# Two-operand scores for strided attention groups, their steps moved into the gate projections, and roots on other engines at both ends

## The chip, the cores and the metric

The kernel runs on one core of one Trainium2 chip. The metric is the device time of one execution in microseconds (us). A core has TensorE (PE in the profile: matmuls and transposes; PEld its weight loads), VectorE (DVE), ScalarE (ACT), GpSimd (POOL) and SyncE (SP, which mainly issues transfers).

## The reference

One layer of an encoder block on 512 tokens of 1024 features, in float32. All weights are read once.

```python
x = x + 0.5 * rmsnorm(swiglu(rmsnorm(x, g1), gate1, up1, down1), g2)      # D_FF = 2816
h = rmsnorm(x, g3)
qa, ka, va, qb, kb, vb, gate_a, gate_b = split(h @ w_in)
ya = neighbourhood_attention(qa, ka, va, rpb) @ w_branch_a                 # 8 heads of 64
yb = dilated_mixture(qb, kb, vb, slopes) @ w_branch_b                      # 3 groups of 4 heads of 64
merged = sigmoid(gate_a) * ya + sigmoid(gate_b) * yb
x = x + rmsnorm(merged @ w_out, g4)
x = x + 0.5 * rmsnorm(swiglu(rmsnorm(x, g5), gate2, up2, down2), g6)
```

The dilated mixture has groups 0, 1 and 2 with dilations 1, 4 and 16. Each group computes a softmax over its own keys with a distance bias (`s - slope * distance`), and the three groups of a head position are weighted by a softmax over their log-sums. rmsnorm divides by the root of the mean square over the 1024 features.

## The kernel before

**Numbers in two parts.** Every matmul operand is split into a rounded high part (ScalarE: a copy that rounds) and a low part (VectorE: source minus high part); `split` does both. `mm3` (lines 203 to 205) multiplies high by high, high by low and low by high. A projection of one 128-feature piece over all tokens is 8 x 3 matmuls with 512 moving columns (`proj_into`).

**Order.** The program is written as one stream; a planner (the framework's scheduler, with a simulated timeline) then orders the instructions of each engine and places waits. In a few stretches PE, ScalarE and VectorE are pinned to the written order (`ordered`): from the start to the first standard pair of the first feed-forward, around the end of the feed-forward and mixing stages, and at the end of the kernel. Elsewhere the planner may move an instruction ahead of others that aren't ready. SBUF work tiles come from one pool of 54 units of 128x512 (`unit`), PSUM tiles from a pool of 8 banks (`bank`), and weight pieces from a pool of 12.

**Start.** Four token tiles of x (128 tokens each) are loaded. For tiles 0 and 1 the sum of squares comes from ScalarE (and for one half of tile 0 from VectorE), then GpSimd adds epsilon and raises to the power -0.5 (`start`, lines 1477 to 1490), VectorE scales (`scaled`), PE transposes (`turned`, line 314) and ScalarE and VectorE write the high and low parts of `hn` (lines 317 and 318). A few matmuls on an idle tile keep PE's clock up (`keep_warm`, counts in `WARM`).

**Feed-forward.** `first_products` runs four products over the first 256 tokens while tiles 2 and 3 are still being turned (`turn_rows`); each turned tile keeps its PSUM bank until `keep` (line 325) has copied it once more into the "whole" tiles. These copies are queued in `kept` and, before the change, run behind the fourth product. Then come two standard projections and `seven`, a seven-product scheme over blocks of two features. `down` is the same for the way back, and `rows_out` normalises, adds and, in the last stage, stores.

**Mixing.** Projections of queries and keys alternate with attention steps that wait in a queue `pend`; `step(n)` takes n steps off it. For each head there is a score step (`scores`, through `g_sc` for the dilated groups), a transpose step (`g_tr`: scales the probabilities, then PE transposes, line 1049) and a value step (`g_pv`, `attend`). `joint(g)` reads the statistics of all three groups back from memory and computes the weights that `g_tr` scales by; the statistics are written by a transfer on ScalarE's queue when a group's last head has been scored. In groups 1 and 2 a block of 128 queries has 128 keys: per block one matmul with the keys' high part and one with their low part, 128 moving columns each, into one quarter of a bank (lines 1017 and 1018). Then VectorE adds the bias table and takes the minimum, and ScalarE takes the exponential. In group 0 and in the neighbourhood attention a block has 256 keys.

Before the change, the steps taken around the far and near values (`v_far`, `v_near`) and a last `step(len(pend))` empty `pend` before the gates. The 16 gates (`gate`, one projection and a sigmoid on ScalarE each) then carry 26 transpose, weight and value steps, two behind each gate from the second on. After them the branch product (`br`) sums ten features' worth of heads per output piece: heads of the neighbourhood attention are rows 0 to 3, group 0 rows 4 and 5, group 1 rows 6 and 7, group 2 rows 8 and 9.

**End.** The last token tile gets its root from GpSimd (`rstd_of`); VectorE does three of the four last multiplies, ScalarE and GpSimd the fourth, and SP and ScalarE issue two stores each.

Of the kernel before, what the change touches and what calls it, by code (L numbers as in the profile page):

```python
# [40 lines left out]
WARM = (0, 1, 0, 1, 9, 2)  # L41
# [4 lines left out]
def block_kernel(ctx, tc, x, gains, weights, rpb_near, rpb_all, alibi0, alibi12, out):  # L46
# [21 lines left out]
    def bank(name="ps"):  # L68
        return pp.tile([P, 512], F32, tag="ps", name=name)
# [47 lines left out]
    staged = {}  # L117
    loads = deque()
# [12 lines left out]
    def convert(n, raw=None):  # L131
        if n in staged:
            hi, lo = [wp.tile([P, PIECE], F32R, tag="w", name="w") for _ in range(2)]
            for u, cs in zip(staged.pop(n), halves):
                split(hi[:, cs], lo[:, cs], u)
# [118 lines left out]
    def first_products(turns, early):  # L254

        w = [take(False) for _ in range(EARLY)]
# [3 lines left out]
        for i in range(EARLY):  # L260
# [11 lines left out]
            if i in turns:  # L272
                turn_rows()
                fetch()
            g = unit(name="g")
# [3 lines left out]
        while kept:  # L279
            kept.popleft()()  # L280
# [18 lines left out]

    def pre_norm(t, g, ss):  # L300
# [5 lines left out]
        late.append(lambda: [turned(t, b, xs[b]) for b in range(2)])  # L306

# [168 lines left out]
    def rows_out(acc, ks, turn, one, ends, g_post, f, g_pre, store, src=None, pin=True):  # L476
# [23 lines left out]
        for tb in complete:  # L500
            squares_of(*tb)
        for tb in complete:
            weighted(*tb)
# [5 lines left out]
        for t in range(NT):  # L509
# [11 lines left out]
            r = rstd_of(ss[t], f)  # L521
            if store and t == NT - 1:

                for b, i in ((1, 0), (0, 0), (0, 1), (1, 1)):
                    part = slice(i * 256, i * 256 + 256)
                    g, o = fg[t][b][:, part], xu[t][b][:, part]
                    if b > i:
                        nc.scalar.mul(g, g, r)
                        nc.gpsimd.tensor_tensor(o, g, o, op=ALU.add)
                    else:  # L530
                        nc.vector.scalar_tensor_tensor(o, g, r, o, op0=ALU.mult, op1=ALU.add)
                for b, i in ((0, 0), (0, 1), (1, 0), (1, 1)):
                    c0 = b * 512 + i * 256
                    (nc.sync, nc.scalar)[i].dma_start(out_r[:, t, c0:c0 + 256], xu[t][b][:, i * 256:i * 256 + 256])
# [11 lines left out]
    def ffn(g, store, src):  # L546
# [34 lines left out]
        if store:  # L581
            nc.scalar.activation(small("ms"), mhalf, AF.Silu)
# [302 lines left out]
    def qk_parts(kind, pq, pk):  # L885
# [3 lines left out]
        for par in range(2):  # L889
            own = slice(par * 64, par * 64 + 64)  # L890
            other = slice(64 - par * 64, 128 - par * 64)
            q, kh, kl = unit(F32R), unit(F32R), unit(F32R)
# [4 lines left out]
            for cols, v in order_k(kind, pk[own]):  # L897
                split(shaped(kh[own, cols], v), shaped(kl[own, cols], v), v)
# [17 lines left out]
    def v_near():  # L916
# [13 lines left out]
        for n in (1, 2, 3, 0):  # L930
# [8 lines left out]
            step()  # L939
        return [vv[3]] + vv[:3]  # L940

    def v_far(g):
# [13 lines left out]
        for n in range(4):  # L956
# [4 lines left out]
            if n % 2:  # L961
                step()
# [35 lines left out]
    def windows(wide, kT, i):  # L998
        if not wide:
            return kT[:, i * P:(i + 1) * P]  # L1000
# [659 lines left out]
```

## Time and profile before

| what | value |
|---|---|
| median of 3 runs | 1087.01 us (1086.24 to 1088.82) |
| the profiled execution | 1087.04 us, span 1085.3 us |
| granted clock of TensorE | 0.999 |
| busy | PE 99%, PEld 89%, DVE 77%, ACT 61%, POOL 17% |
| chain that ended last | PE 93%, DVE 2%, DMA 2%, ACT 1% |
| DMA | 189.82 MB, mean 175 GB/s |

Times in a timeline are microseconds from the span's start. A row of the timeline has start, length, engine, line, operation, output<-inputs, shape and count, and in brackets how long the engine was idle before it and what ended that. Lengths of matmuls are modelled and overlap; what a matmul costs PE is read from one start to the next. A row of the waits says who waited at which line for whom: total us, times, longest. A row of the groups has count, busy us, mean ns of one, and idle time before them. A row of the windows gives, for a stretch, busy us and instructions of PE, PEld, DVE, ACT and POOL, then the granted clock, the DMA share and GB/s.

### The profile page before, as it was taken

To read this page: it belongs to the slowest core of one execution; us is meant where nothing else is said; L and a number is where in the kernel's file an instruction comes from. 1 tells how busy PE (TensorE), PEld (TensorE's weight loads), DVE (VectorE), ACT (ScalarE), POOL (GpSimd) and SP (SyncE) were. 2 spreads that over 40 slices of the span, in tenths; PEclk is the share of its full clock that TensorE was granted. 3 is DMA by queue.
4 is the path that set the end of the run, shared out by engine and by line. 5 is a ranking of instruction groups with operands and counts; after the bars stand their busy time and mean duration, and the time that the engine had idled before them with its cause. 6 is when DMAs were issued, how large, how long until landed. Compare 5 with 4: busy or idle time off the path is not lost.

```text
span 1085.3 us, 18420 instructions
## 1 busy us (share of the span) xinstructions
PE 1073.0 (99%) x6689; PEld 967.6 (89%) x6689; DVE 834.2 (77%) x1561; ACT 657.1 (61%) x1334; POOL 182.2 (17%) x252
## 2 busy tenths in 40 slices
PE   8999999999999999999999999999999999999997
PEld 6899999998888988888988888889899999998876
DVE  7988777768997679876467654777988777778975
ACT  7646555565784767767656651376656555565762
POOL 4112111014333000000000001133302111114301
PEclk9999999999999999999999999999999999999999
DMA  9889997569993353422232239666928767859962
GB/s 338 184 202 248 225 233 186 143 160 280 237 292 98 127 194 109 134 87 79 70 103 79 79 111 304 161 113 207 277 64 211 190 162 188 203 184 240 218 199 77
DMA packets 95725, 189.82 MB, mean 175 GB/s; under 512 B 24081, under 2 KB 26641, under 8 KB 95634
## 3 DMA queue, kind: packets, MB, share of 16 engines
q1 hardware_dynamic: 68320, 134.18, 37.1%
q0 software_dynamic: 24624, 54.01, 27.6%
q8 instruction: 52, 0.85, 0.3%
q10 hardware_dynamic: 2690, 0.46, 0.2%
q14 instruction: 39, 0.32, 0.1%
HBM read 183.58 MB, written 7.58 MB: 176 GB/s over the span
## 4 chain that ended last, share of the span: by engine, by line
PE 93%; DVE 2%; DMA 2%; ACT 1%; issue 1%; POOL 0%; SPq 0%; DVEq 0%; POOLq 0%; ACTq 0%
PE ps L203 11%; PE ps L204 11%; PE ps L205 11%; PE q L203 10%; PE q L204 10%; PE q L205 10%; PE p L203 4%; PE p L204 3%; PE p L205 3%; PE r L205 2%; PE r L204 2%; PE r L203 2%; PE c L205 2%; PE c L204 2%; PE c L203 2%; PE ps L1049 1%
## 5 line engine op out<-in xcount | busy, mean ns | idle before, releaser
L113 DVE TENSOR_TENSOR w<-raw,w 128x512 fp32r<-128x512 f32 (+1 forms) x136 | 122.9, 909 | 69.7 <-ACT w L112 69.4
L112 ACT CAST w<-raw 128x512 fp32r<-128x512 f32 (+1 forms) x136 | 107.8, 799 | 83.5 <-PE ps L204 41.9
L203 PE MATMUL ps<-hn,w 128*128 128x512 f32 (+1 forms) x408 | 155.5, 381 | 2.3 <-ACT whole L325 2.3
L205 PE MATMUL ps<-hn,w 128*128 128x512 f32 (+1 forms) x408 | 153.2, 375 | 0.0
L204 PE MATMUL ps<-hn,w 128*128 128x512 f32 (+1 forms) x408 | 153.1, 375 | 0.0
L113 DVE TENSOR_TENSOR w<-t,w 128x512 fp32r<-128x512 f32 x160 | 108.9, 688 | 20.9 <-ACT w L112 18.4
L112 ACT CAST w<-t 128x512 fp32r<-128x512 f32 x160 | 97.6, 619 | 42.8 <-DVE t L380 24.3
L203 PE MATMUL p<-v,w 128*128 128x256 f32 x320 | 90.6, 283 | 0.3 <-ACT up L454 0.3
L203 PEld LDWEIGHTS ps<-hn,w 128*128 128x128 f32 x408 | 76.9, 189 | 15.3 <-ACT whole L325 2.7
L203 PE MATMUL q<-v,w 128*128 128x256 f32 x320 | 90.6, 283 | 0.0
L204 PE MATMUL p<-v,w 128*128 128x256 f32 x320 | 90.5, 283 | 0.0
L204 PE MATMUL q<-v,w 128*128 128x256 f32 x320 | 90.5, 283 | 0.0
L205 PE MATMUL p<-v,w 128*128 128x256 f32 x320 | 90.2, 283 | 0.0
L205 PE MATMUL q<-v,w 128*128 128x256 f32 x320 | 89.9, 283 | 0.0
L205 PEld LDWEIGHTS ps<-hn,w 128*128 128x128 f32 x408 | 76.8, 188 | 14.0
L204 PEld LDWEIGHTS ps<-hn,w 128*128 128x128 f32 x408 | 77.0, 189 | 12.5
L374 POOL DMA_DIRECT2D t<-in_weights_dram x40 | 35.0, 875 | 287.4 <-DVE w L113 85.3
L204 PE MATMUL q<-hn,w 128*128 128x256 f32 x288 | 81.5, 283 | 0.0
L205 PE MATMUL q<-hn,w 128*128 128x256 f32 x288 | 81.5, 283 | 0.0
L203 PE MATMUL q<-hn,w 128*128 128x256 f32 x288 | 81.3, 283 | 0.0
L203 PE MATMUL q<-w,a 128*128 128x512 f32 x192 | 75.0, 391 | 0.6 <-DVE part L831 0.6
L204 PE MATMUL q<-w,a 128*128 128x512 f32 x192 | 74.7, 389 | 0.0
(269 smaller groups left out, 3018.6 us busy)
## 6 DMA issues: line engine op xcount, KB each, us to landing
raw<-in_weights_dram SPq DMA_DIRECT2D x90, 512.0 KB
t<-in_weights_dram SPq DMA_DIRECT2D x88, 256.0 KB
t<-in_weights_dram POOLq DMA_DIRECT2D x80, 256.0 KB, 5.6
w<-in_weights_dram SPq DMA_DIRECT2D x40, 256.0 KB
rows<-in_weights_dram SPq DMA_DIRECT2D x32, 256.0 KB
w<-in_weights_dram POOLq DMA_DIRECT2D x32, 256.0 KB, 6.2
tb<-in_weights_dram POOLq DMA_DIRECT2D x12, 512.0 KB, 8.5
rows<-in_weights_dram POOLq DMA_DIRECT2D x24, 256.0 KB, 11.3
```

Source lines behind the costliest of these rows:

```text
L112: nc.scalar.copy(hi, src)
L113: nc.vector.tensor_tensor(lo, src, hi.bitcast(F32), op=ALU.subtract)
L203: nc.tensor.matmul(o, sh, mh, start=start, stop=False, **kw)
L204: nc.tensor.matmul(o, sh, ml, start=False, stop=False, **kw)
L205: nc.tensor.matmul(o, sl, mh, start=False, stop=stop, **kw)
L374: nc.gpsimd.dma_start(t1, weights[gate][:, :512], accum_op=ALU.add)
L1049: nc.tensor.transpose(ps[:, i * P:(i + 1) * P], s, ident)
```

## The change

1. **Scores of groups 1 and 2** (`scores_narrow`): the keys of two query blocks lie in one tile, high parts in its first half and low parts in its second. One matmul per block with 256 moving columns (128 high, 128 low) gives both products side by side. VectorE adds the low products and the bias table into a new tile `low`, then adds the high products and takes the minimum. A head now takes 4 matmuls instead of 8 and two banks instead of one.
2. **Steps**: `v_near` takes two steps instead of four, the second part of `v_far` none, and `pend` isn't emptied before the gates. Four steps (scores of three heads of group 2, and `joint(1)`) move behind gates 1 and 2, and the others two gates later. The branch product takes rows 4 and 5 last.
3. **Turned tokens**: at the start all transposes come before the copies out of PSUM, and the copies are ordered by half: both tiles' first halves, then the second (`turned_first`). The `keep` copies run behind a turn inside `first_products` instead of behind the fourth product.
4. **Roots**: tiles 0 and 1 and the last tile of the kernel get their root from ScalarE (`Sqrt`) and a reciprocal on VectorE, instead of GpSimd's power. The first table load is that of Sqrt; the Silu load moves behind the first turn of the first feed-forward, and another Sqrt load is placed ahead of the last stage's tail. At the end VectorE does all four multiplies, each followed by its store.
5. **Smaller ones**: the low half of one staged weight piece moves to GpSimd; the row of gains and the ones it is multiplied by get 128 rows (zeros but for one) instead of one; the warm-up counts grow.

The diff, cut to its core:

```diff
@@ -38,7 +38,7 @@
 EXTRA = "e"
-WARM = (0, 1, 0, 1, 9, 2)
+WARM = (1, 2, 1, 1, 10, 3)
 PINNED = (mybir.EngineType.PE, mybir.EngineType.Activation, mybir.EngineType.DVE)
@@ -253,6 +256,8 @@
+        if turns[0] == 0:
+            nc.scalar.activation(small("ms"), mhalf, AF.Silu)
         w = [take(False) for _ in range(EARLY)]
@@ -272,12 +277,14 @@
                 fetch()
+                if i == 1:
+                    nc.scalar.activation(small("ms"), mhalf, AF.Silu)
+                while kept and i != 1:
+                    kept.popleft()()
             g = unit(name="g")
             early.append((o, g))
-        while kept:
-            kept.popleft()()
@@ -297,6 +304,14 @@
+    def root_of(ss, f):
+        c, m, r = small("ms0"), small("ms"), small("rstd")
+        nc.gpsimd.tensor_scalar_add(c, ss[:, 0:1], f * EPS)
+        nc.scalar.activation(m, ss[:, 1:2], AF.Sqrt, bias=c)
+        nc.vector.reciprocal(r, m)
+        return r
     def pre_norm(t, g, ss):
@@ -304,6 +319,18 @@
         late.append(lambda: [turned(t, b, xs[b]) for b in range(2)])
+    def turned_first(t, b, xs):
+        pt = bank()
+        for i in range(4):
+            nc.tensor.transpose(pt[:, i * P:(i + 1) * P], xs[:, i * P:(i + 1) * P], ident)
+        to = (slice(None), slice(4 * b, 4 * b + 4), slice(t * P, (t + 1) * P))
+        pt = pt.rearrange("p (k t) -> p k t", t=P)
+        def copies():
+            nc.scalar.copy(hn_hi[to], pt)
+            nc.vector.tensor_tensor(hn_lo[to], pt, hn_hi[to].bitcast(F32), op=ALU.subtract)
+        return copies
@@ -499,6 +526,8 @@
             squares_of(*tb)
+        if store:
+            nc.scalar.activation(small("ms"), ss[NT - 1][:, 0:1], AF.Sqrt)
         for tb in complete:
@@ -518,20 +547,15 @@
                         weighted(t, b)
-            r = rstd_of(ss[t], f)
+            r = (root_of if store and t == NT - 1 else rstd_of)(ss[t], f)
             if store and t == NT - 1:
-                for b, i in ((1, 0), (0, 0), (0, 1), (1, 1)):
-                    part = slice(i * 256, i * 256 + 256)
-                    g, o = fg[t][b][:, part], xu[t][b][:, part]
-                    if b > i:
-                        nc.scalar.mul(g, g, r)
-                        nc.gpsimd.tensor_tensor(o, g, o, op=ALU.add)
-                    else:
+                for b in (1, 0):
+                    for i, queue in enumerate((nc.sync, nc.scalar)):
+                        part = slice(i * 256, i * 256 + 256)
+                        g, o = fg[t][b][:, part], xu[t][b][:, part]
                         nc.vector.scalar_tensor_tensor(o, g, r, o, op0=ALU.mult, op1=ALU.add)
-                for b, i in ((0, 0), (0, 1), (1, 0), (1, 1)):
-                    c0 = b * 512 + i * 256
-                    (nc.sync, nc.scalar)[i].dma_start(out_r[:, t, c0:c0 + 256], xu[t][b][:, i * 256:i * 256 + 256])
+                        queue.dma_start(out_r[:, t, b * 512 + i * 256:b * 512 + i * 256 + 256], o)
                 continue
@@ -889,13 +911,19 @@
             other = slice(64 - par * 64, 128 - par * 64)
-            q, kh, kl = unit(F32R), unit(F32R), unit(F32R)
+            q, kh, kl = unit(F32R, "q"), unit(F32R, "k"), unit(F32R, "k")
             v = seen(kind, pq[own])
             nc.vector.scalar_tensor_tensor(qx, v, 0.125, qo.bitcast(F32), op0=ALU.mult, op1=ALU.subtract)
-            for cols, v in order_k(kind, pk[own]):
-                split(shaped(kh[own, cols], v), shaped(kl[own, cols], v), v)
+            if kind in (1, 2):
+                v = seen(kind, pk[own])
+                for i, u in enumerate((kh, kl)):
+                    part = v[:, 2 * i:2 * i + 2]
+                    split(shaped(u[own, :256], part), shaped(u[own, 256:], part), part)
+            else:
+                for cols, v in order_k(kind, pk[own]):
+                    split(shaped(kh[own, cols], v), shaped(kl[own, cols], v), v)
             nc.vector.tensor_copy(kh[other], kh[own].bitcast(F32))
@@ -936,7 +964,8 @@
             vv.append(v_parts(ps[:, :256]))
-            step()
+            if n in (0, 2):
+                step()
         return [vv[3]] + vv[:3]
@@ -958,8 +987,6 @@
             vv.append(v_parts(ps[:, :256]))
-            if n % 2:
-                step()
         yield vv
@@ -995,18 +1022,40 @@
-    def windows(wide, kT, i):
-        if not wide:
-            return kT[:, i * P:(i + 1) * P]
+    def windows(kT, i):
         if i < 3:
-    def scores(wide, parts, table, st, h):
+    def scores_narrow(parts, table, st, h):
+        q, ks = parts[0], parts[1:]
+        p = unit()
+        for b in range(2):
+            ps = bank()
+            for i in range(2):
+                k = ks[b].rearrange("p (s n t) -> p n s t", s=2, n=2)[:, i]
+                nc.tensor.matmul(ps[:, i * 256:(i + 1) * 256], q[:, (2 * b + i) * P:(2 * b + i + 1) * P], k,
+                                 start=True, stop=True)
+            low = unit(name="low")
+            o = ps.rearrange("p (n s t) -> p n s t", n=2, s=2)
+            nc.vector.tensor_tensor(low[:, :256].rearrange("p (n t) -> p n t", n=2), o[:, :, 1],
+                                    table.unsqueeze(1).to_broadcast([P, 2, P]), op=ALU.add)
+            for n in range(2):
+                i = 2 * b + n
+                nc.vector.tensor_tensor_reduce(
+                    out=p[:, i * P:(i + 1) * P], in0=o[:, n, 0], in1=low[:, n * P:(n + 1) * P], scale=-1.0,
+                    scalar=3.0e38, op0=ALU.add, op1=ALU.min, accum_out=st[:, i, h, 0:1])
+            for i in (2 * b, 2 * b + 1):
+                s = slice(i * P, (i + 1) * P)
+                nc.scalar.activation(p[:, s], p[:, s], AF.Exp, bias=st[:, i, h, 0:1], scale=-1.0,
+                                     accum_out=st[:, i, h, 1:2])
+        return [p]
+    def scores(parts, table, st, h):
         q, kh, kl = parts
-        w = 256 if wide else 128
-        per = 512 // w
+        w, per = 256, 2
         prob = []
@@ -1217,8 +1266,10 @@
         def g_sc(g, parts, h):
-            tab = table_of(g_tab[h // 2], h) if g == 0 else lambda i: g_tab[g + 1][0][:, h * P:(h + 1) * P]
-            hold["p", g, h] = scores(g == 0, parts[h % 2], tab, st[g], h)
+            if g == 0:
+                hold["p", g, h] = scores(parts[h % 2], table_of(g_tab[h // 2], h), st[g], h)
+            else:
+                hold["p", g, h] = scores_narrow(parts[h % 2], g_tab[g + 1][0][:, h * P:(h + 1) * P], st[g], h)
             if h == 3:
@@ -1259,7 +1310,6 @@
         vvb[2] = next(far[1])
-        step(len(pend))
         seq = [(g, h) for g in (1, 2, 0) for h in range(4)]
@@ -1341,12 +1391,12 @@
             ya, yb = bank(), bank()
-            for k in range(10):
+            for k in (0, 1, 2, 3, 6, 7, 8, 9, 4, 5):
                 i, c = divmod((f * 10 + k) * P, PIECE)
                 mm3(ya if k < 4 else yb, *cut(br[i], c, P), o_parts[k][0], o_parts[k][1],
-                    k in (0, 4), k in (3, 9))
+                    k in (0, 6), k in (3, 5))
             m1, m2 = unit(), unit()
@@ -1474,37 +1526,36 @@
-    def start(t, shared):
-        ms, r = small("ms"), small("rstd")
-        ss = small("ssx", 2)
-        sumsq(xu[t][0], ss[:, 0:1])
-        if shared:
-            nc.vector.tensor_tensor_reduce(out=unit(name="junk"), in0=xu[t][1], in1=xu[t][1], scale=1.0 / D,
-                                           scalar=EPS, op0=ALU.mult, op1=ALU.add, accum_out=ss[:, 1:2])
-            nc.gpsimd.tensor_scalar(ms, ss[:, 0:1], ss[:, 1:2], None, op0=ALU.add)
-        else:
-            sumsq(xu[t][1], ss[:, 1:2])
-            nc.gpsimd.tensor_scalar(ms, ss[:, 0:1], ss[:, 1:2], EPS, op0=ALU.add, op1=ALU.add)
-        nc.gpsimd.tensor_tensor(r, ms, mhalf, op=ALU.pow)
-        rs[t] = r
-    start(0, True)
+    def root(t, sq, bias):
+        m, rs[t] = small("ms"), small("rstd")
+        nc.scalar.activation(m, sq, AF.Sqrt, bias=bias)
+        nc.vector.reciprocal(rs[t], m)
+    for t in range(2):
+        ss[t] = small("ssx", 2)
+    sumsq(xu[0][0], ss[0][:, 0:1])
+    nc.vector.tensor_tensor_reduce(out=unit(name="junk"), in0=xu[0][1], in1=xu[0][1], scale=1.0 / D,
+                                   scalar=EPS, op0=ALU.mult, op1=ALU.add, accum_out=ss[0][:, 1:2])
+    root(0, ss[0][:, 0:1], ss[0][:, 1:2])
     scaled(0, 0)
     scaled(0, 1)
-    start(1, False)
+    part = small("ms0")
+    sumsq(xu[1][0], ss[1][:, 0:1])
+    nc.gpsimd.tensor_scalar_add(part, ss[1][:, 0:1], EPS)
+    sumsq(xu[1][1], ss[1][:, 1:2])
+    root(1, ss[1][:, 1:2], part)
     scaled(1, 0)
     split_piece(0, 0, True)
+    turns = []
+    for n, (t, b) in enumerate(((0, 0), (0, 1), (1, 0), (1, 1))):
+        turns.append(turned_first(t, b, xs[t, b]))
+        keep_warm(n)
+    turns[0]()
+    turns[2]()
     split_piece(0, 1, True)
-    turned(0, 0, xs[0, 0])
-    keep_warm(0)
-    turned(0, 1, xs[0, 1])
-    keep_warm(1)
-    turned(1, 0, xs[1, 0])
-    keep_warm(2)
-    turned(1, 1, xs[1, 1])
-    keep_warm(3)
+    turns[1]()
+    turns[3]()
     split_piece(1, 0)
```

Left out are the conversions of the one staged piece, the zeroed rows at the start, the naming of tiles, and calls that only follow the new signatures.

More of the change, by code (lines that the diff above doesn't have):

```diff
@@ L117, in block_kernel @@
     staged = {}
+    shared = {EARLY}
     loads = deque()
@@ L580, in ffn @@
         early = []
-        if store:
-            nc.scalar.activation(small("ms"), mhalf, AF.Silu)
         first_products((0, 2) if store else (1, 2), early)
@@ L1016, in scores @@
                 cols = slice(i * P, (i + 1) * P)
-                nc.tensor.matmul(ps[:, o:o + w], q[:, cols], windows(wide, kh, i), start=True, stop=False)
-                nc.tensor.matmul(ps[:, o:o + w], q[:, cols], windows(wide, kl, i), start=False, stop=True)
+                nc.tensor.matmul(ps[:, o:o + w], q[:, cols], windows(kh, i), start=True, stop=False)
+                nc.tensor.matmul(ps[:, o:o + w], q[:, cols], windows(kl, i), start=False, stop=True)
             for i in range(b * per, (b + 1) * per):
@@ L1170, in na_sc @@
             s4 = sp.tile([P, 4, 1, 2], F32, tag="nast", name="nast", bufs=4)
-            pr = scores(True, parts[h % 2], table_of(na_tab[h // 2], h), s4, 0)
+            pr = scores(parts[h % 2], table_of(na_tab[h // 2], h), s4, 0)
             rc = sp.tile([P, 4], F32, tag="narc", name="narc", bufs=4)
@@ L1412, in block_kernel @@
     ordered.append([mark()])
-    silu = small("ms")
+    root = small("ms")
     idle = unit(BF16, name="idle")
     nc.vector.memset(idle, 0.0)
-    row, row_hi, row_lo = [wp.tile([P, PIECE], dt, tag="w", name="row")[0:1] for dt in (F32, F32R, F32R)]
+    row, row_hi, row_lo = [wp.tile([P, PIECE], dt, tag="w", name="row") for dt in (F32, F32R, F32R)]
+    nc.vector.memset(row_hi.bitcast(F32), 0.0)
+    row, row_hi1, row_lo1 = row[0:1], row_hi[0:1], row_lo[0:1]
     nc.scalar.dma_start(row, gains[0:1, :])
@@ L1419, in block_kernel @@
     load_x(1, x_r)
-    nc.scalar.activation(silu, mhalf, AF.Silu)
-    ones = const.tile([1, P], F32, name="ones")
-    ones_r = const.tile([1, P], F32R, name="ones_r")
+    nc.scalar.activation(root, mhalf, AF.Sqrt, scale=-1.0)
+    ones = const.tile([P, P], F32, name="ones")
+    ones_r = const.tile([P, P], F32R, name="ones_r")
     nc.gpsimd.memset(ones, 1.0)
+    nc.gpsimd.memset(row_lo.bitcast(F32), 0.0)
     nc.vector.tensor_copy(ones_r, ones)
-    nc.vector.tensor_copy(row_hi, row)
-    nc.vector.tensor_tensor(row_lo, row, row_hi.bitcast(F32), op=ALU.subtract)
+    nc.vector.tensor_copy(row_hi1, row)
+    nc.vector.tensor_tensor(row_lo1, row, row_hi1.bitcast(F32), op=ALU.subtract)
     raws = []
```

4 lines of the change are left out of this document (3 added, 1 removed).

## The prediction

> **What bounds the kernel now.** I read the page first, then who waits for whom on PE, then single stretches of the timeline around each edited line.
>
> ```profile
> PE 1073.0 (99%) x6689; PEld 967.6 (89%) x6689; DVE 834.2 (77%) x1561; ACT 657.1 (61%) x1334; POOL 182.2 (17%) x252
> PE 93%; DVE 2%; DMA 2%; ACT 1%; issue 1%; POOL 0%; SPq 0%; DVEq 0%; POOLq 0%; ACTq 0%
> ...
> PE ps L203 <- ACT whole L325: 2.3, 2, 1.3
> PE ps L314 <- DVE u L1465: 1.2, 1, 1.2
> PE q L203 <- DVE part L831: 0.6, 1, 0.6
> ```
>
> PE is busy 99% of the span and is 93% of the chain that ended last. The waits show that, after the first instruction, it stands still for longer in four places only: at the very start (the 1.2 for x's turned tiles), twice for the "whole" copies at the start of a feed-forward stage (2.3 in two waits), and 0.6 near the end. Between about 30 and 1078 us, therefore, a microsecond is won by issuing less PE work or by ending one of those waits, and lost by a new wait. Work on DVE, ACT and POOL counts only where PE ends up waiting for it.
>
> The profiled execution took 1087.04 us for a span of 1085.3, so 1.7 us lie around the span; the median of the runs is 1087.01, practically the same, and I make the sum against 1087.0. About 0.2% (2.2 us) is what a measurement of this kernel can tell from no change.
>
> **Part 1: scores of the strided groups.** Eight heads (groups 1 and 2) each issue 8 matmuls with 128 moving columns; afterwards they issue 4 with 256. I read what PE pays from one start to the next, since the modelled lengths overlap.
>
> ```profile
> 515.58 0.39 PE L205 MATMUL ps<-hn,w 128*128 128x512 f32 x1
> 515.80 0.22 PE L1017 MATMUL ps<-u 128*128 128x128 f32 x1
> ...
> 516.64 0.45 PE L203 MATMUL ps<-hn,w 128*128 128x512 f32 x1
> ...
> 576.26 0.64 PE L1085 MATMUL ps<-u 128*128 128x256 f32 x4
> 576.73 0.49 PE L1049 MATMUL ps<-ident,u 128*128 128x128 f32 x3
> ```
>
> One narrow head runs from 515.80 to 516.64: 0.84 us. (A projection's matmul takes 0.22 to 0.23, 515.58 to 515.80.) Line 1085 already issues the new form, four matmuls with 256 moving columns taken as two runs of 128: 576.26 to 576.73, 0.47 us. So 0.37 a head, 8 x 0.37 = 3.0 us off PE. If a 256-column matmul were no better here than two narrow ones, the gain would be 0; I take 3.0, because line 1085 is the same shape and the same stride.
>
> The price is on DVE, ACT and in PSUM. A head adds two sums into "low" and fills two banks where it filled one.
>
> ```profile
> L1021 DVE CUSTOM_DVE_ANT_0 u<-ps,table 128x128 f32<-128x128 f32 x32 | 7.4, 286 | 14.2 <-PE ps L1018 14.2
> L1090 DVE TENSOR_TENSOR u<-ps,u 128x256 f32<-128x256 f32 x16 | 6.0, 414 | 1.4 <-ACT u L1089 1.4
> 515.00:547.00 32.00, 32.00 (x228) 29.85 (x227) 14.79 (x83) 22.19 (x88) 0.00 (x0) 1.00 0.23 65
> 547.00:640.00 93.00, 93.00 (x475) 79.08 (x474) 66.34 (x156) 58.35 (x98) 0.00 (x0) 1.00 0.29 87
> ```
>
> At 0.41 a sum (line 1090, also a bank read and added) that is 0.83 us of DVE a head, 6.6 in all; splitting the keys in two halves instead of one adds a few short instructions. DVE works 14.79 of 32 us where the scores run now (515 to 547) and 66.34 of 93 in the gates (547 to 640), so the idle time covers it. Without this cover it would be at most the 6.6.
>
> **Part 2: steps moved into the gates.** Four steps leave the near and far values: the scores of three heads of group 2, and the joint weights of group 1. They are now queued behind gates 1 and 2, and everything after them moves two gates later; the last step lands behind gate 15, where nothing was before. PE work is the same. The last two heads of group 0 are then needed by the branch product, but their rows now come last of each sum, after 8 x 3 matmuls of line 203 to 205, so that cover exists. What the move puts at risk is the path from the last score to the first scaled probability.
>
> ```profile
> 543.23 0.28 PE L1018 MATMUL ps<-u 128*128 128x128 f32 x1
> 545.57 0.52 ACTq L1223 DMA_DIRECT2D stats<-st  x1
> 550.73 0.18 DVE L1207 TENSOR_TENSOR joint<-joint 128x16 f32<-128x16 f32 x1 [0.87 <-DMA joint<-stats]
> 553.50 0.88 DVE L1037 TENSOR_SCALAR u<-u,joint 128x128 f32<-128x128 f32 x4
> 553.66 1.28 ACT L1276 ACT_TABLE_LOAD   x1
> ...
> 438.98 0.38 PE L1049 MATMUL ps<-ident,u 128*128 128x128 f32 x2
> 442.85 0.81 PE L1049 MATMUL ps<-ident,u 128*128 128x128 f32 x6
> ```
>
> From 543.51 (end of the last score) through the statistics' way to memory and back to the end of the scaling at 554.38 it took 10.9 us. In the new place the path also has the two sums (0.8) and, because sigmoids now stand between the exponentials, two table loads of 1.28: 14.3 us. PE has one gate to do meanwhile, 24 matmuls of 0.23, 5.5 us. In strict program order PE would stand 8.8 us. But the order is a planner's, and the rows at 438.98 and 442.85 show it put two of a head's eight transposes ahead and six behind part of a projection: it moves PE work past what isn't ready. With one more gate moved ahead the wait is 3.3, with two it is none. Bounds 0 and 8.8; I take 0.4, near the lower end, because PE had no wait in the whole mixing stage although such pieces are placed there without a margin.
>
> ACT gets three heads' exponentials and about four more table loads in the gates. The Trainium skill (ScalarE: Activation LUTs, "Table sets: the hidden batching unit") tells authors to finish all calls of one table set before the next and speaks against this spreading; by its 2.66 us for a switch the path above would be 17.0 instead of 14.3. The trace has 1.28 for the load and the sigmoid follows within 0.02 of it (553.66 to 554.96), so I keep the row's.
>
> **Part 3: start and first feed-forward.**
>
> ```profile
> 2.60 0.20 ACT L1420 ACTIVATE ms<-mhalf 128x1 f32<-128x1 f32 x1
> 7.34 0.19 ACT L285 ACTIVATION_READ_ACCUMULATOR junk<-x 128x1 f32 x1
> 8.60 1.41 DVE L1465 SCALAR_TENSOR_TENSOR u<-x,rstd,gain 128x512 f32<-128x512 f32 x2 [1.35 <-POOL rstd L1489]
> 10.74 1.22 PE L267 MATMUL q<-hn,w 128*128 128x256 f32 x8
> L1173 DVE RECIPROCAL narc<-nast 128x4 f32<-128x4 f32 x8 | 1.4, 172 | 2.2 <-ACT u L1026 2.1
> ...
> 21.12 1.07 ACT L317 CAST hn<-ps 128x512 fp32r<-128x512 f32 x2 [1.35 <-PE ps L314]
> 24.69 1.21 ACT L325 COPY whole<-ps 128x256 f32<-128x256 f32 x4
> 25.40 0.50 PE L203 MATMUL ps<-hn,w 128*128 128x512 f32 x1 [1.01 <-ACT whole L325]
> ```
>
> The second tile's sum of squares is read at 7.53 and DVE scales at 8.60: 1.07 by way of POOL's power. A root on ACT (0.20, as the 128x1 activation at 2.60) and a reciprocal (0.17, line 1173) with hand-overs are about 0.4: DVE starts 0.65 earlier, and so do the transposes. The first product also needs only the first halves' copies now, instead of all four, and the POOL part of the first piece. But both roots sit in ACT's queue ahead of its casts, so the later squares come about 0.4 later and the next tokens' turn eats half: 0.3 stays. The added warm-up matmuls and the zeroed rows run while x is under way; at worst 0.2 each.
>
> PE's restart at 25.40 waits for the copies that free two banks. They now stand behind one cast pair instead of the last product's g copies; but Silu's table load (1.28 + 0.20) moves into the same queue. ACT's idle 1.35 ahead of 21.12 covers most of it. I take 0.3 off the wait, so 0.6 for the start in all. Bounds: minus 1.7 (0.65 and the whole 1.01) to plus 0.5 (load and roots, 1.9, less the idle 1.35). The low half of piece 4 goes from DVE to POOL and frees DVE there; POOL's queued additions by DMA start later, for blocks first needed after two projections.
>
> **Part 4: second feed-forward.**
>
> ```profile
> 760.26 0.94 ACT L325 COPY whole<-ps 128x256 f32<-128x256 f32 x3
> 760.98 0.50 PE L203 MATMUL ps<-hn,w 128*128 128x512 f32 x1 [1.31 <-ACT whole L325]
> ```
>
> Here the third tile's copies move behind the first product, more than 4 us before PE wants their banks, and the table load stays where it was. The wait goes: minus 1.4 (1.31 and the slow restart). What is late next is DVE's low half of the last tile, which has that product's time. Bounds minus 1.5 and 0.
>
> **Part 5: the end.**
>
> ```profile
> 1079.34 0.19 ACT L285 ACTIVATION_READ_ACCUMULATOR junk<-q 128x1 f32 x1
> 1079.57 0.69 DVE L497 TENSOR_TENSOR u<-q,gain 128x512 f32<-128x512 f32 x1 [1.56 <-ACT junk L285]
> 1080.67 0.88 DVE L531 SCALAR_TENSOR_TENSOR x<-u,rstd,x 128x256 f32<-128x256 f32 x2 [0.41 <-POOL rstd L297]
> 1081.58 1.21 ACTq L534 DMA_DIRECT2D out_y_dram<-x  x2
> ```
>
> The root is ready before DVE ends the weighting (1080.26); the reciprocal makes it 1080.45 instead of 1080.67. Then four multiplies on DVE instead of three. Two took 0.88 here, so four are 1.7, ending at 1082.15, and a last issue of 0.34 ends at 1082.5 instead of 1082.79: minus 0.3. If all four were as slow as the row's three with POOL beside them the end would be 0.3 later; POOL has nothing there now, so I take minus 0.3. The new table load for the root, early in this stage, is on ACT among casts made several steps ahead: nothing.
>
> **Sum.** -3.0 + 0.4 - 0.6 - 1.4 - 0.3 = -4.9, so 1087.0 - 4.9 = 1082.1 us.
>
> **Rivals.**
> 1. The joint weights come late (the other side). PE stands behind the first transposes of group 1. For it: 14.3 us of path against 5.5 of program-order cover, and DVE already waited 0.87 for the landing of these statistics, so the planner counted on them sooner. Against it: PE never waited in this stage. Gain without it 5.3; beyond 5.3 of wait the change loses, beyond 3.1 it can't be told from nothing. In program order: 1087.0 - 5.3 + 8.8 = 1090.5; with one gate ahead 3.3, 1085.0.
> 2. The waits at both feed-forward starts stay, bound by ACT's longer queue: only scores and end remain, 1087.0 - 3.0 - 0.3 + 0.4 = 1084.1.
> 3. The square isn't in the root's table set, so loads alternate at both ends: two on the start's path and one at the end, 3 x 1.28 = 3.8 more: 1085.9. Against it: the waits and groups of before show no load at line 285.
>
> **Chances.** Forecast 0.58 (own range 1080.7 to 1083.6); rival 1 with 2 to 5 us of wait 0.16, with more 0.09; rival 2 0.12; rival 3 0.05. Faster by over 0.2%: 0.58 + 0.12 + a third of the 0.16 = 0.75. Slower by over 0.2% needs 7.5 us of wait: 0.08. The rest, 0.17, is within. The range reaches from 1080.7 (the start and the waits at their good ends) to 1086.0, which takes in rivals 2 and 3 and rival 1 up to about 4 us of wait.
>
> **What would show it.** Right: scores at four matmuls in about 0.48 us, no wait of PE for line 325 copies near 760, a restart before 25.4, a last issue 0.3 sooner after PE's end, no PE wait in the gates. Wrong: PE idle ahead of line 1049's transposes about two gates after the last narrow score; table loads beside line 285; the first product no earlier than 10.74.

## The result and the profile after

The changed kernel takes 1093.89 us (median of 4 runs, 1093.53 to 1094.5), the kernel before 1087.38 (1086.24 to 1088.82): a ratio of 1.0062, with an interval of 1.0049 to 1.0074. The change costs some 6.5 us where the forecast had 4.9 off.

The profiled execution took 1093.57 us for a span of 1091.8. In the changed file the projections' matmuls stand at lines 206 to 208 (203 to 205 before), the transposes of the probabilities at 1098 (1049), the strided scores at 1038, the "whole" copies at 352 (325). Engines, then the chain that ended last:

```profile
PE 1073.0 (98%) x6662; PEld 966.5 (89%) x6662; DVE 841.9 (77%) x1588; ACT 668.3 (61%) x1354; POOL 182.2 (17%) x249
PE 93%; DMA 2%; DVE 2%; ACT 2%; issue 0%; SPq 0%; DVEq 0%; ACTq 0%
```

The busy time of PE is the same to the tenth, with 27 instructions fewer; the share fell from 99 to 98%. The time is in waits, so the next view is who PE waited for (total, times, longest, in us):

```profile
PE ps L1098 <- DVE u L1086: 7.3, 1, 7.3
...
PE ps L1098 <- ACT sig L1326: 0.9, 1, 0.9
...
PE ps L206 <- ACT whole L352: 0.8, 1, 0.8
PE ps L988 <- DVE st L1046: 0.6, 1, 0.6
PE ps L1098 <- DVE u L1139: 0.4, 1, 0.4
```

One wait of 7.3 us, ahead of a transpose: there was none in this stage before. Of the two "whole" waits one is left. The small ones at lines 1098 and 988 are new. PE's timeline around the large one:

```profile
566.11 0.39 PE L208 MATMUL ps<-hn,w 128*128 128x512 f32 x1
573.83 0.45 PE L1098 MATMUL ps<-ident,u 128*128 128x128 f32 x1 [7.33 <-DVE u L1086]
573.93 0.78 PE L206 MATMUL ps<-hn,w 128*128 128x512 f32 x1
...
577.92 0.49 PE L206 MATMUL ps<-hn,w 128*128 128x512 f32 x1
```

The last matmul of gate 3 starts at 566.11, and then one single transpose stands at the head of PE's queue until 573.83. It is 7.7 us from start to start where 0.23 is usual: 7.5 lost. The projection behind it needs nothing of that transpose, but it starts only behind it (573.93). What follows runs at 0.43 from start to start instead of 0.23 until 577.9; about ten matmuls and the odd ones after them lose 2.1 us more. The windows give the reason; the third figure from the end is the granted clock:

```profile
566.00:574.00 8.00, 0.67 (x5) 0.27 (x3) 3.50 (x15) 4.75 (x7) 0.00 (x0) 0.83 0.29 80
574.00:578.00 4.00, 4.00 (x11) 3.13 (x11) 2.62 (x14) 0.00 (x0) 0.00 (x0) 0.50 0.00 0
578.00:582.00 4.00, 4.00 (x21) 3.25 (x20) 0.52 (x2) 0.85 (x3) 0.00 (x0) 0.98 0.00 0
```

PE counts as busy for all of 574 to 578 and does half the work there, 11 matmuls against 21. A busy share would never show it; the clock column does.

What PE waited for is followed back in the chain, cut to this stretch (start, length):

```profile
560.37 1.05 ACT w L112
561.44 1.28 ACT L1326
562.74 0.60 ACT sig L1326
563.35 1.28 ACT L1051
564.65 1.66 ACT u L1051 x8
566.33 2.04 DMA stats<-st
568.39 0.34 ACTq L1253
568.77 1.28 ACT L1326
...
570.67 1.28 ACT L1260
571.97 0.25 ACT joint L1260
...
573.40 0.30 DVE u L1086
573.83 0.45 PE ps L1098
```

From the last narrow score (560.87, where the next matmul starts) to the transpose (573.83) it is 13.0 us. Four of these pieces are table loads of 1.28 (those at lines 1326, 1051 and 1260 that carry no tile). PE had one gate to do meanwhile, 560.87 to 566.3.

Among the groups of the gates' stretch (547 to 645 us), the loads of after, and of before in the second fence:

```profile
L1326 ACT ACT_TABLE_LOAD x6 | 7.7, 1283 | 0.9 <-DMA stats<-st 0.8
L1260 ACT ACT_TABLE_LOAD x3 | 3.8, 1283 | 0.1
L1051 ACT ACT_TABLE_LOAD x2 | 2.6, 1283 | 0.0
```

```profile
L1276 ACT ACT_TABLE_LOAD x3 | 3.8, 1283 | 0.1
L1211 ACT ACT_TABLE_LOAD x2 | 2.6, 1283 | 0.0
```

Eleven loads instead of five, where the forecast had about four more. Elsewhere the profile after has what the forecast said. A strided head on PE, and the third tile's copies in the second feed-forward:

```profile
515.26 0.64 PE L1038 MATMUL ps<-k,q 128*128 128x256 f32 x4
515.73 0.40 PE L206 MATMUL ps<-hn,w 128*128 128x512 f32 x1
```

```profile
763.60 1.20 ACT L352 COPY whole<-ps 128x256 f32<-128x256 f32 x4
```

The head takes 0.47. The copies start more than 4 us ahead of the projection that wants their banks (768.3), and PE no longer stands there. The end:

```profile
1085.36 0.39 PE L208 MATMUL q<-w,a 128*128 128x512 f32 x1
...
1087.17 0.15 DVE L312 RECIPROCAL rstd<-ms 128x1 f32<-128x1 f32 x1
1087.36 1.67 DVE L557 SCALAR_TENSOR_TENSOR x<-u,rstd,x 128x256 f32<-128x256 f32 x4
1088.27 1.14 ACTq L558 DMA_DIRECT2D out_y_dram<-x  x2
```

From PE's last end (1085.75) to the last issue's end (1089.41) it is 3.66 us; before it was 4.04 (1078.75 to 1082.79). The four multiplies take 1.67.

### The profile page after: what moved, and what is told of

Its sections match the earlier page's. It is cut to its first block, busy times and chain, and to the rows that moved or that the text cites. A ratio compares the mean times of both kernels' runs of the same rounds, so it can differ in the third digit from the quotient of the medians.

```text
span 1091.8 us, 18436 instructions
## 1 busy us (share of the span) xinstructions
PE 1073.0 (98%) x6662; PEld 966.5 (89%) x6662; DVE 841.9 (77%) x1588; ACT 668.3 (61%) x1354; POOL 182.2 (17%) x249
## 4 chain that ended last, share of the span: by engine, by line
PE 93%; DMA 2%; DVE 2%; ACT 2%; issue 0%; SPq 0%; DVEq 0%; ACTq 0%
PE ps L206 11%; PE ps L207 10%; PE ps L208 10%; PE q L206 10%; PE q L208 10%; PE q L207 10%; PE p L206 4%; PE p L208 4%; PE p L207 4%; PE r L208 3%; PE r L206 3%; PE r L207 3%; PE c L207 2%; PE c L208 2%; PE c L206 2%; DMA raw<-in_weights_dram 2%
## 5 line engine op out<-in xcount | busy, mean ns | idle before, releaser
L113 DVE TENSOR_TENSOR w<-raw,w 128x512 fp32r<-128x512 f32 (+1 forms) x120 | 112.6, 939 | 68.8 <-ACT w L112 67.1
L112 ACT CAST w<-raw 128x512 fp32r<-128x512 f32 (+1 forms) x120 | 98.7, 822 | 73.7 <-PE ps L207 34.8
```

The lines of the kernel that those rows point to most:

```text
L112: nc.scalar.copy(hi, src)
L113: nc.vector.tensor_tensor(lo, src, hi.bitcast(F32), op=ALU.subtract)
```

## Experiments

The kernel before took between 1086.4 and 1087.9 us (medians) on the chips used, so kernels are compared by their ratio to it on the same chip, with a 95% interval; gains in us are that ratio against 1087. Each edit also lets the planner order the rest anew, so a time can hold more than the edit; the rows say what waits came with it.

**Undo the step move alone, and do it alone.** If the missing cover is the cause, both directions must show it.

The first kernel is the changed one with the steps of the near values, of the far values and the flush ahead of the gates as they were:

```diff
-            if n in (0, 2):
-                step()
+            step()
...
+            if n % 2:
+                step()
...
+        step(len(pend))
```

> The changed kernel with its steps put back where they were (in the near and far values, the rest flushed ahead of the gates); all other parts kept. Theory W (PE stands behind the first transposes of group 1, which wait for the joint weights, and then runs at a lowered clock for some us: 7.5 + 2.2 us in the changed kernel's profile): the wait and the slow stretch go, 1093.9 - 9.7 = about 1084.2 us, between 1082.5 and 1085.5. Rival S (the new score form itself, with its two sums and two banks a head, is what delays PE wherever it stands): it stays above 1090.

Measured 1083.16 us, ratio 0.9964 (0.9952 to 0.9977). With the steps back the change is worth 3.9 us; with them in the gates it costs 6.7. No wait is left in the gates. One new wait stands among the far values; the row is of this kernel's PE timeline:

```profile
531.86 0.48 PE L1039 MATMUL ps<-k,q 128*128 128x256 f32 x2 [1.55 <-DVE st L1047]
```

PE waits in the middle of the third of three heads that follow each other within 2 us. A head holds two banks now, and VectorE had not read the earlier ones.

The second is the kernel before with the same edits the other way round, and with the branch sum's rows 4 and 5 last:

```diff
-            step()
+            if n in (0, 2):
+                step()
...
-            if n % 2:
-                step()
...
-        step(len(pend))
...
-            for k in range(10):
+            for k in (0, 1, 2, 3, 6, 7, 8, 9, 4, 5):
```

> The kernel before with only the steps moved into the gates (and the last two heads' rows last in the branch sums); old scores, roots and copies. Theory W: the path to the first scaled probability is 0.8 us shorter without the two sums, so PE waits about 6.7 us at the same place and loses some 2 us to the clock: 1087.4 + 8.7 = about 1096 us (1094 to 1097.5). Rival S: without the new scores there is no wait, 1087 to 1088.5.

Measured 1099.9 us, ratio 1.0122 (1.0104 to 1.0141): 13.3 slower, more than expected, though the old scores are in it.

```profile
PE ps L1048 <- DVE u L1036: 8.1, 1, 8.1
```

The same wait at the same place, with no sums on the path; so the placement makes it, not the new scores. The wait (8.2 us from start to start), the slow clock behind it (2.8) and the last gate's waits of 1.8 us for ACT's sigmoid and DVE's value sum, the same as in the changed kernel, make 12.8 of the 13.3. That the path did not get shorter (13.8 us from the last score to the transpose, counted as above) is a miss of mine. The chain shows why: in both kernels the path from the last score goes through ScalarE's sigmoid, its loads and the exponentials, so the two sums weren't on it. Here ScalarE also does a cast of weights behind the read of the statistics, and in the changed kernel ahead of it, beside the write (566.95):

```profile
571.46 1.04 ACT L112 CAST w<-raw 128x1024 fp32r<-128x1024 f32 x1 [2.61 <-DMA stats<-st]
```

**Give the path more cover.** Three kernels keep the steps in the gates, but begin earlier and leave a pause between the joint weights and the first transpose.

Two gates of cover (e3):

```diff
-            if f:
+            if f != 2:
                 step(2)
```

> The changed kernel with one more gate between the joint weights and the first transposes of group 1: the steps begin one gate earlier (behind gate 0), none behind gate 2, all after as they were. Theory W: the wait is the path of 13.0 us less 5.45 a gate, so 7.5 - 5.4 = 2.1 us is left, and 0.5 to 2 us of slow clock: 1093.9 - 5.4 - (0.2 to 1.7) = 1087.0 to 1088.5. Rival T (the path grows with the number of gates in it, since each sigmoid brings two more table loads on ScalarE and so the weights stay just as late): 1092 to 1094.

Measured 1089.56 us, ratio 1.0024 (1.0014 to 1.0034).

```profile
570.48 0.30 PE L1098 MATMUL ps<-ident,u 128*128 128x128 f32 x1 [2.89 <-DVE u L1086]
```

The wait fell by 4.4 us for one gate of 5.45. The path had grown from 13.0 to 14.0 us (556.51 to 570.48): two heads behind one gate keep ScalarE longer, and the statistics leave 6.4 us behind the last score instead of 5.5. The lowered clock followed this shorter pause too; the window is of the first 4 us behind it:

```profile
570.00:574.00 4.00, 3.52 (x10) 2.87 (x11) 3.96 (x18) 1.69 (x2) 0.00 (x0) 0.63 0.00 0
```

Three gates (e4):

```diff
-            if f:
-                step(2)
+            if f not in (2, 3):
+                step(3 if f in (7, 10) else 2)
```

> As the one before with two more gates of cover: steps behind gates 0 and 1, none behind 2 and 3, three instead of two behind 7 and 10. Theory W: 13.0 us of path against 16.3 of gates, no wait and no slow clock: 1093.9 - 9.7 = about 1084.2 us (1083 to 1085.5). Rival T: 1090 to 1094.

Measured 1090.32 us, ratio 1.003 (1.0021 to 1.004). The first wait is gone, as theory W has it, and yet the time is no better than with two gates. Another wait has come:

```profile
PE ps L1098 <- ACT sig L1326: 3.9, 2, 3.0
```

I put that down to the three steps bunched behind gate 7, and tried it without (e14):

```diff
-            if f:
+            if f not in (2, 3):
                 step(2)
```

> The changed kernel with two more gates of cover as in the run before of that kind, but two steps behind every later gate and what is left (two last values of group 0) behind gate 15, ahead of the branch product. Theory W with the bunching as the cause of that run's later wait: neither wait, 1093.9 - 9.7 = 1084.2 us, up to 1085.5 if the flush costs its own wait at the end (ratio to before 0.998 to 0.999). Rival T (the steps in the gates cost PE as much wherever they are put): 1090 (ratio 1.003).

Measured 1097.94 us, ratio 1.0092 (1.0076 to 1.0107): slower than both, so the bunching alone is not it. The first transposes again do not wait. But PE loses 1.9, 1.8, 1.8 and 1.8 us at later ones, and 3.5 plus a slow stretch of 2.6 at the branch product, whose values were flushed just ahead of it. Its VectorE and ScalarE timelines show a likely source of the first of these, and the third row the same block in e4, ahead of the wait of 3.0:

```profile
590.40 4.29 DVE L1086 TENSOR_SCALAR u<-u,joint 128x256 f32<-128x256 f32 x16
596.25 0.37 ACT L112 CAST u<-ps 128x256 fp32r<-128x256 f32 x1 [5.12 <-DVE u L113]
591.75 4.29 DVE L1086 TENSOR_SCALAR u<-u,joint 128x256 f32<-128x256 f32 x16
```

The sixteen scalings of group 0, all four heads, stand in one block of 4.3 us in VectorE's queue. A gate's weights and the low part that ScalarE's next cast waits for (5.12 us idle) come behind it, and behind that cast the sigmoid that PE then waits for. In the changed kernel the sixteen are broken up. Both chains run through this block; that it is the cause was not tested.

So the missing cover makes the wait of 7.5 us: it is 7.3, 2.9 and 0 in the profile's count with one, two and three gates. But cover alone doesn't bring the time back: each of the schedules tried that fills all the gates with steps pays somewhere else in them.

**What the table loads have in it.** Exp instead of Sigmoid in the gates needs no other table; this kernel leaves out the sigmoid, so its values differ.

```diff
-            nc.scalar.activation(s, o, AF.Sigmoid)
+            nc.scalar.activation(s, o, AF.Exp)
```

> The changed kernel with Exp in place of Sigmoid in the 16 gates (the sigmoid is left out, so the values differ; the same count and shape of instructions), which takes the table loads out of the gates. Theory L (the loads lengthen the path from the last narrow score to the first scaled probability): two loads of 1.28 ahead of the exponentials and some 1.2 of the one ahead of the joint exponential go, the wait falls from 7.5 to 3.7 us and the slow stretch shrinks a little: 1093.9 - 3.8 - 0.4 = 1089.7 us (1088.3 to 1090.7). Rival (the loads lie beside the statistics' way to memory and cost nothing): 1092.5 or more.

Measured 1092.26 us, ratio 1.0052 (1.0039 to 1.0066): 1.8 us off the path (11.2 instead of 13.0), half of what I expected. ScalarE's timeline, with the idle time ahead of a piece in brackets:

```profile
564.95 0.52 ACTq L1274 DMA_DIRECT2D stats<-st  x1
566.83 1.04 ACT L112 CAST w<-raw 128x1024 fp32r<-128x1024 f32 x1 [1.92 <-PE ps L207]
567.99 0.34 ACTq L1253 DMA_DIRECT2D joint<-stats  x1
```

Counted from the end of the last score (561.39 here), the statistics leave 1.9 us earlier than in the changed kernel (3.56 against 5.46). But the read of the joint statistics is issued by ScalarE, behind a cast that waits 1.92 us for PE and ends at 567.87. So only 0.9 of it reaches that issue (6.60 against 7.52). The other 0.9 comes off the load ahead of the joint exponential. The Trainium skill (ScalarE: Activation LUTs, "Table sets: the hidden batching unit") says to batch activations by table set, and the direction holds here. The 2.66 us that the Trainium skill gives for a switch (same page, "What ACT_TABLE_LOAD costs") do not, as a load takes 1.28 and the sigmoid follows 0.02 later (561.44, 562.74).

**The clock.** Matmuls on zeros fill the pause.

```diff
+            if f == 3:
+                busy = bank("busy")
+                for _ in range(32):
+                    nc.tensor.matmul(busy, filler[:, :P], filler, start=True, stop=True)
             if f:
                 step(2)
```

> The changed kernel with 32 matmuls on zeros (128x512, bfloat16, about 0.21 us each, 6.8 us in all) behind gate 3, where PE otherwise stands still for 7.5 us. Theory C (the granted clock is halved for some 4 us after the idle stretch, because PE was idle): the wait is as long but filled, the projections behind it take 0.23 instead of 0.43, 1093.9 - 2.1 = 1091.8 us. Rival (the clock falls for another reason, or the filling only delays): 1093.9 or more, 0.43 each as before.

Measured 1094.37 us, ratio 1.0074 (1.006 to 1.0088).

```profile
575.38 0.30 PE L1098 MATMUL ps<-ident,u 128*128 128x128 f32 x1 [0.97 <-DVE u L1086]
575.43 0.48 PE L206 MATMUL ps<-hn,w 128*128 128x512 f32 x1
```

```profile
574.00:578.00 4.00, 3.03 (x15) 2.18 (x14) 3.83 (x20) 0.00 (x0) 0.00 (x0) 1.00 0.00 0
```

The mechanism is right: with PE kept busy the clock stays at 1.00 and the matmuls behind at 0.23. The gain is not there. The weights came 13.5 instead of 13.0 us behind the last score, which makes the pause 0.6 longer, and PE loses 0.8 at 601 us where it had not before. That uses up 1.4 of the 2.1 us of slow clock; this profile also reaches the last score 1.0 us later (561.38 against 560.40), for a reason ahead of the gates. Why the weights came later was not traced. The Trainium skill (TensorE: Matmul & The Clock Gate, "What's actually happening") has half rate after an idle window of about 3.4 us, until as long a busy one; the changed kernel's windows agree, 0.50 for some 4 us behind the wait of 7.3, but in e3 a pause shorter than 3.4 us was enough (2.89 of wait).

**The parts one by one,** each on the kernel before, steps in their old places.

e5 has scores_narrow and its split keys, and nothing else of the change. e6 has this, in first_products:

```diff
+                while kept and i != 1:
+                    kept.popleft()()
...
-        while kept:
-            kept.popleft()()
```

e7 has the start (roots, order, warm-up, zeroed rows, the fifth piece's low half on GpSimd), Silu's new place, and the end.

> The kernel before with only the new scores of the strided groups; steps, copies and roots as before. Theory B (two banks a head instead of one; among the short transposes of the far values three heads follow each other and PE waits 2.0 us for a bank, as in the run with the steps put back): 8 x 0.37 = 3.0 us off, 2.0 back, 1086.5 - 1.0 = 1085.5 (1084.7 to 1086.3). Rival (the full 3.0 arrives, the stall belongs to another part): 1083.5.

Measured 1086.29 us, ratio 0.9987 (0.9978 to 0.9996), 1.4 us off. The same 2.0 us are lost at 530 us as in the first experiment; theory B holds.

> The kernel before with only the copies of the turned tokens moved ahead of the last product's, in both feed-forward stages. Theory: the wait at the second feed-forward's start goes (1.4 us), the first one's stays (the run with the steps put back still shows 0.9 there): 1086.5 - 1.4 = 1085.1 (1084.5 to 1085.8). Rival (ScalarE is the bound at both starts, the wait comes back with another name): 1086.5.

Measured 1084.86 us, ratio 0.998 (0.9971 to 0.999), 2.2 us off. Both waits for the "whole" copies are gone, the first feed-forward's too; that one I had wrong.

> The kernel before with only the start (roots, order of the first turned tokens, warm-up, the fifth piece's low half on GpSimd) and the end (root and four multiplies). Theory: about 0.4 at the end and 0 to 0.6 at the start: 1085.5 to 1086.1. Rival (GpSimd's 3.0 us low half beside VectorE slows VectorE's turned rows, and eats the start's gain): no gain but the end's, 1086.1 to 1086.4.

Measured 1087.06 us, ratio 1.0 (0.9991 to 1.0008). Start and end together give nothing, and the end by itself gives 0.4 in the trace.

**Better placements.** e8 is e1 with one step less among the far values; the last head then comes behind the near values and the joint weights behind the second far values.

```diff
-            if n % 2:
+            if n == 3:
                 step()
...
-        step(len(pend))
```

> The changed kernel with the steps out of the gates as in the first run, but only one instead of two among the transposes of the first far values; the last head comes behind the near values, the joint weights behind the second far values. Theory B (the 2.0 us stall is bank shortage from three heads close together): the stall goes, 1083.2 - 2.0 = 1081.2 (1080.7 to 1082). Rival (VectorE as such is late there, the stall only moves): 1083.

Measured 1082.79 us, ratio 0.9965 (0.9953 to 0.9978), no better than e1. The stall at 530 is gone, and PE waits 1.6 for the first scaled probability at 555 instead: the joint weights are late again. The next two move those steps ahead and not behind; e11 has the old start (and the old order of rows in the branch product), e12 the changed one. The edit, against e1:

```diff
-    def pair(use, j, n=2):
+    def pair(use, j, n=2, extra=0):
...
-        step(n)
+        step(n + extra)
...
-            pair(g_use, j, 1 if j else 3)
+            pair(g_use, j, 1 if j else 3, j in (2, 4))
...
-            if n % 2:
-                step()
```

> The kernel before with the new scores, the moved copies and the end's roots, but the old start; no step in the gates. The steps that stood among the far values' transposes come earlier, one extra behind the first projection of the third and of the fifth strided pair, so no three heads are close together and the joint weights are not later than in the first run. Theory: 3.0 + 2.2 (the copies alone took 2.2) + 0.4 off, and no stall of 2.0 at the far values: 1086.5 - 5.6 = about 1080.9 us (1080 to 1082.3). Rival (the 2.0 us only move again, as they did when the last head went behind the near values): 1082.9.

Measured 1081.14 us, ratio 0.9947 (0.9934 to 0.9961), 5.8 us off, as expected. There is no stall at the far values and none in the gates.

> The same with the changed start as well (that is, the changed kernel with all steps out of the gates, and the two extra ones earlier). Theory P (the start gives nothing: the gain ahead of the first product is lost again where PE waits 0.9 at the first feed-forward's restart, a wait that the copies alone take away): 0 to 1 us slower than the kernel with the old start, 1081 to 1082. Rival (the start is worth the 0.6 of the prediction): 0.6 faster than it, about 1080.3.

Measured 1082.03 us, ratio 0.9952 (0.9939 to 0.9964), which can't be told from e11's by the intervals. The trace tells where the start goes wrong. With the old start PE restarts 13.5 us after the first product (11.08 to 24.57), with the new one 15.1 (10.06 to 25.14). In the changed kernel, VectorE, GpSimd, ScalarE and PE:

```profile
20.20 2.98 DVE L1525 TENSOR_TENSOR w<-raw,w 128x512 fp32r<-128x512 f32 x2
```

```profile
19.65 2.99 POOL L137 TENSOR_TENSOR w<-raw,w 128x512 fp32r<-128x512 f32 x2 [0.81 <-DVE u L1517]
```

```profile
24.90 1.18 ACT L352 COPY whole<-ps 128x256 f32<-128x256 f32 x4
```

```profile
25.59 0.50 PE L206 MATMUL ps<-hn,w 128*128 128x512 f32 x1 [0.77 <-ACT whole L352]
```

Two subtractions take VectorE 2.98 us beside GpSimd's two. What ScalarE's next activation waits for stands behind them, and behind that the copies that PE waits for. The last experiment is e12 with one edit:

```diff
-    shared = {EARLY}
+    shared = set()
```

> The run with all steps out of the gates and the changed start, but the low half of the fifth piece back on VectorE (it was put on GpSimd by the change). Theory P (GpSimd's 2.99 us beside VectorE's two subtractions, 2.98 where the old start has 1.28, delays the turned rows of the fourth tile and with them the copies that PE's restart waits for, 24.90 against 23.78): from the first product to PE's restart 15.07 becomes about 13.9 us, and the time falls by about 1.1: ratio to before 0.9942, some 1080.4 us where before has 1086.5. Rival (Silu's table load at the restart is what delays it): 15.0 still, no change, 0.9952.

Measured 1080.87 us, ratio 0.9933 (0.992 to 0.9947), the best of all, 7.3 us off. From this kernel:

```profile
19.90 1.28 DVE L1525 TENSOR_TENSOR w<-raw,w 128x512 fp32r<-128x512 f32 x2
```

```profile
24.48 0.50 PE L206 MATMUL ps<-hn,w 128*128 128x512 f32 x1 [0.42 <-ACT whole L352]
```

The subtractions are back at 1.28, and from the first product (10.21) to the restart it is 14.3 us instead of 15.1, of the 13.9 expected. The wait left, 0.42, may come from Silu's load, which stands in ScalarE's queue ahead of the casts; it wasn't tried. e12 and e13 were timed on different chips, and their intervals overlap slightly, so the step between them is shown by the rows rather than by the ratios.

## Why the prediction was wrong

**The step that failed: the joint-weights wait, "Bounds 0 and 8.8; I take 0.4".** Both of its measures were good: 14.3 us of path (measured 13.0, as the first transpose needs one of the four scalings and not all) and 5.5 of cover (5.45). That the path fits is partly luck: the forecast added the two sums, which weren't on it (e2), and two table loads, where the chain after has four. The program-order end was therefore nearly the truth, 8.8 against 7.5. What was wrong is the reason for the other end: "it moves PE work past what isn't ready". The planner did that before the kernel ran, on its simulated timeline, and put the first transpose ahead of the next projection and the other three behind part of it. When the kernel ran the order stood; one transpose, 0.1 us from its start to the next, held up everything behind it. That PE "never waited" in this stage before was evidence for the old placement, with 14.6 us of PE work between the last score and the first transpose (543.5 to 558.1), and none for the new one, with 5.5. Rival 1 at its program-order value is what happened, at 0.09 for more than 5 us of wait.

**What no term of the sum had.** The lowered clock behind the pause: 2.1 us on PE. The last step behind gate 15: the sum noted that nothing was there before and charged nothing, and PE waits for gate 15's own sigmoid and for the value sum, 1.8 us from start to start. The second bank of a head: "Without this cover it would be at most the 6.6" looked at VectorE's idle share and not at banks; PE loses 1.2 us at 541 in the changed kernel (e2, with the old scores, has no wait there), and 2.0 at 530 in e1 and e5.

**Scores, -3.0.** Right on PE, 0.47 a head. Net of the banks 1.4 (e5).

**Start and first feed-forward, -0.6.** From the second tile's last square to PE's restart it was 17.87 us before (7.53 to 25.40) and is 17.83 (7.76 to 25.59): nothing. Three sizes were off. VectorE scales 0.62 after the square instead of 1.07, which is 0.45 earlier and not 0.65. The moved copies alone take the whole 1.0 off the restart (e6), not 0.3. And "the low half of piece 4 goes from DVE to POOL and frees DVE there" is the wrong way round: it cost VectorE 1.7 us just ahead of the fourth tile's rows.

**Second feed-forward, -1.4, and the end, -0.3.** Right: the wait is gone, and the end is 0.38 shorter. Rival 2 came half true, by a cause it didn't name. Rival 3 did not come: no table load stands beside the squares.

**The new sum** against the two profiles, which lie 6.5 us apart: -3.0 for the scores, +1.2 for banks, +9.6 for the joint weights with the slow clock, +1.8 behind gate 15, 0 at the start (+0.2 with x's own landing), -1.5 and -0.4 for the second feed-forward and the end, close to the forecast, and about -0.9 from small waits of before (at 233 and 1055 us) that shrank: +7.0, some 0.5 over the difference. Undone alone, the step move accounts for all of the loss and more (e1).

## What to carry to other kernels

A wait for a value that is formed through another engine, memory and back is priced by the program order of the in-order queues, even where a planner arranges them: count the work that really stands between the last producer and the first consumer in the new order, and ask for at least the path's length. Work spread into a stage that looks idle shares its ScalarE and VectorE queues with that stage's own chain; here every way tried of putting these four steps more into the gates cost PE time, and with the same steps earlier, behind the strided pairs' projections, PE had no wait (e11). An instruction moved to GpSimd frees VectorE only if VectorE can run beside it; here it could not (e13).

## What the runs showed of the hardware

Two of VectorE's subtractions of 128x512 tiles in SBUF take 1.28 us alone (e13) and 2.98 beside the same on GpSimd, which took 2.99 for its two. The Trainium skill (SBUF — State Buffer, "Who interferes with whom") says that a VectorE instruction with two SBUF inputs contends with a GpSimd instruction that reads SBUF, and the rows agree.

A pause of about 3 us was enough for the lowered clock (e3: 2.89 of wait, then a granted clock of 0.63 over 570 to 574 us); pauses of 1.6 us (e1, e8) were followed by none. By short windows the clock fell some 4.8 us after PE's last matmul had ended in the changed kernel, 3.4 in e3 and 2.8 in e4; in e3 that was half a microsecond after PE had started again.

Filling a pause kept the clock up (1.00) and gained nothing on the whole (e10: ratio 1.0074, against 1.0062 for the changed kernel).
